# A two-path decoder trunk on one core: the place of a transposition in the last chunk of each feed-forward block, and the pace of a bias table's transfers

## The chip, the cores and the metric

The kernel runs on one core of a Trainium2 chip. The metric is the device time of one execution in microseconds (us), the median of several runs. One further execution was recorded by the hardware profiler; all rows come from it. The engines are TensorE (PE; its weight loads are shown apart as PEld), VectorE (DVE), ScalarE (ACT), GpSimd (POOL) and SyncE (SP, which here only starts transfers). Each has its own queue of instructions and works through it in order.

## The reference, cut to what matters

Two layers over 256 tokens of width 1024. Each layer adds half a feed-forward block (ffn), then a mixer, then half of another ffn. The mixer of the first layer is a diagonal state-space model (S5), that of the second is an attention with three branches over keys and values computed between the layers.

```python
def _swiglu(x, w_in, w_out):
    a, b = jnp.split(x @ w_in, 2, axis=-1)
    return (jax.nn.silu(a) * b) @ w_out
...
for layer in range(DEPTH):
    h = h + 0.5 * _swiglu(_rmsnorm(h, ffn1_norm[layer]), ffn1_w_in[layer], ffn1_w_out[layer])
    u = _rmsnorm(h, mix_norm[layer])
    ...
    h = h + 0.5 * _swiglu(_rmsnorm(h, ffn2_norm[layer]), ffn2_w_in[layer], ffn2_w_out[layer])
    if layer == N_A_LAYERS - 1:
        kv = _shared_kv(...)
```

So four ffns are computed, each with an inner width of 2816. The attention adds to its scores a bias that depends only on the distance of query and key, through 32 buckets of a table `rel_bias` with 16 heads.

## The kernel before

**Products in three passes.** Every float32 matrix is split into a high part (`whi`, rounded, by ACT at L86 or L99) and a low part (`wlo`, the rest, by DVE at L90 or L102; a few by POOL). A product is then three matmuls in `mm3` (L115 to L120): high by high (L118), high by low weights (L119), low by high (L120). Weights come from DRAM as `raw` tiles of 1 MB by `load_granule` (L68), started from SP. `raw` has two buffers, `whi` and `wlo` five of 1024 columns each, so splits run ahead of the matmuls until a buffer is missing.

**A feed-forward block** (`ffn`, L191) goes over 11 chunks (NCH) of 256 inner columns. For each chunk c it computes both halves of the first product for the two token tiles t into two PSUM banks `mm` (48 matmuls over eight k), then `g` = silu(a) * b (ACT L249, DVE L250, for t = 0 and 1). The second product needs `g` with the inner columns on the partitions. `transposed(g)` (L198) does that with four PE transposes (L204) into one bank `tr`, which `split` (L142) copies to `gT` as a high part (ACT L143) and a low part (DVE L144). In the second ffn (`perm`) the split goes in two halves. `second(c, gT)` (L214) then adds 24 matmuls into the four banks `o`: two inner halves f, two output halves hf, two t, three passes. The work is skewed by one chunk: while chunk c's first product runs, the `g` of chunk c - 1 is transposed (after k = 4, L243), and `second(c - 1)` follows the first product of chunk c (L253). After the loop the last chunk is left: L256 transposes its `g` and computes `second(10)`, whose sums L228 adds to `h`; after each sum `done` prepares the next stage.

**The order on each engine.** The source gives each instruction a rank. A scheduler sets the order of each engine's queue when the kernel is built, by rank and by when it expects operands to be ready; on the chip each queue runs in order, with waits on semaphores. An instruction of low rank may thus stand ahead of one of higher rank that was expected to be ready later.

**Background work.** `ffn` can take a generator `bg` with small steps of other work. `background(bg, steps)` (L179) is called after the odd k of each chunk but the first, and at the end of every chunk: call 1 ends chunk 0, and calls 5c - 3 to 5c + 1 lie in chunk c. A step that yields 1 lets the next call go on; a step that yields n counts for n calls. The instructions of a step on ACT, DVE and SP are put behind the latest instructions of the main work on these engines (L185); those on POOL are not.

In the second ffn the background is `bias_tables` (L632). It loads the table and the buckets, multiplies them on PE (L640), and copies the result to `rev` (L643). Then eight transfers, started from POOL, write `rev` 16-fold to a DRAM buffer `revd` (L647, 384 KB each), and one reads it back with overlapping rows as `B` (L652, 2 MB), which the attention uses after the third ffn.

Of the kernel before, what the change touches and what calls it, by code (L numbers as in the profile page):

```python
# [21 lines left out]
NCH = FF // 256  # L22
# [10 lines left out]
def kernel(ctx: ExitStack, tc: tile.TileContext, A, out):  # L33
# [13 lines left out]
    def mm_bank():  # L47
        return Banks.mm.tile([P, 512], F32, name="mm")

    def tr_bank():  # L50
        return Banks.tr.tile([P, 512], F32, name=Banks.tag)
# [55 lines left out]
    def granules(aps, w=512, gain=None, first=(), eng="av"):  # L107
        for n, ap in enumerate(aps):
            raw = first[n] if n < len(first) else load_granule(ap, w)
            for j in range(2):  # L110
                hi, lo = split_half(raw, j, w, gain, ((n % 2) * 2 + j) * 2, eng)
                for s_ in range(2):
                    yield hi[:, s_ * w:(s_ + 1) * w], lo[:, s_ * w:(s_ + 1) * w]

    def mm3(ps, xT, k, t, w, start, stop_):  # L115
        xh, xl = (xT[:, i, k, t * P:(t + 1) * P] for i in range(2))
        wh, wl = w
        T.matmul(ps, lhsT=xh, rhs=wh, start=start, stop=False)  # L118
        T.matmul(ps, lhsT=xh, rhs=wl, start=False, stop=False)  # L119
        Last.pe = T.matmul(ps, lhsT=xl, rhs=wh, start=False, stop=stop_)  # L120

    def gemm(acc, xT, gen, kts=KT, lead=False):

        for k0 in range(0, kts, 4):
            ws = [next(gen) for _ in range(4)] if lead else None
            for t_ in range(2) if lead else (None,):
                for k in range(k0, k0 + 4):
                    w = ws[k - k0] if lead else next(gen)
                    for t in ((t_,) if lead else range(2)):
                        mm3(acc[t], xT, k, t, w, k == 0, k == kts - 1)  # L130
# [11 lines left out]
    def split(dst_hi, dst_lo, src):  # L142
        i = S.activation(dst_hi, src, AF.Copy)  # L143
        V.tensor_tensor(out=dst_lo, in0=src, in1=dst_hi.bitcast(F32), op=ALU.subtract)  # L144
        return i
# [33 lines left out]
    def background(bg, n):  # L179

        if bg is None:
            return
        Pace.left = min(Pace.left, 0.0) + n
        with ExitStack() as st:
            for i in (Last.act, Last.dve, Last.dma):  # L185
                st.enter_context(tc.issue_after(i.ins))
            while Pace.left > 0:
                Pace.left -= next(bg, n) or 1


    def ffn(x, gi, w_in, w_out, res, perm=False, bg=None, steps=1, done=None, first=()):  # L191
        with tc.tile_pool(name="ffn", bufs=2) as fp, tc.tile_pool(name="ps_a", bufs=1, space=PSUM) as pa:
            xT, rs = x.xT, x.rs
            acc2 = [[pa.tile([P, 512], F32, name=f"o{t}{hf}") for hf in range(2)] for t in range(2)]
            g_in = granules([w_in[c, kh] for c in range(NCH) for kh in range(2)], gain=gi, first=first)
            g_out = granules([w_out[j] for j in range(NCH)])

            def transposed(g):  # L198

                gT = fp.tile([P, 2, 2, 256], F32R, name="gT")  # L200
                ps = tr_bank()
                for f in range(2):
                    for t in range(2):
                        T.transpose(ps[:, (f * 2 + t) * P:(f * 2 + t + 1) * P], g[:, t, f * P:(f + 1) * P], ident)  # L204
                if perm:
                    src = ps.rearrange("p (f t e c) -> p f t e c", f=2, t=2, e=2)
                    hi, lo = (gT[:, i].rearrange("p f (c t e) -> p f t e c", t=2, e=2) for i in range(2))
                    for f in range(2):
                        split(hi[:, f], lo[:, f], src[:, f])
                else:  # L210
                    split(gT[:, 0], gT[:, 1], ps.rearrange("p (f c) -> p f c", f=2))
                return gT

            def second(c, gT):  # L214
                if c < NCH - 1:
                    for f in range(2):
                        for hf in range(2):
                            w = next(g_out)
                            for t in range(2):
                                mm3(acc2[t][hf], gT, f, t, w, c + f == 0, False)  # L220
                    return
                ws = [[next(g_out) for _ in range(2)] for _ in range(2)]
                for t in range(2):
                    for hf in range(2):
                        for f in range(2):
                            mm3(acc2[t][hf], gT, f, t, ws[f][hf], False, f == 1)
                        cs = slice(hf * 512, (hf + 1) * 512)
                        V.scalar_tensor_tensor(out=res[:, t, cs], in0=acc2[t][hf], scalar=0.5, in1=res[:, t, cs], op0=ALU.mult, op1=ALU.add)  # L228
                        done(t, hf)

            prev = None
            for c in range(NCH):
                acc = [mm_bank() for _ in range(2)]
                gT = None
                if c == 0:
                    gemm(acc, xT, g_in, lead=True)
                else:
                    for k in range(KT):
                        w = next(g_in)
                        for t in range(2):  # L240
                            mm3(acc[t], xT, k, t, w, k == 0, k == KT - 1)
                        if k == 4:
                            gT = transposed(prev)  # L243
                        if k % 2:
                            background(bg, steps)
                g = fp.tile([P, 2, 256], F32, name="g")
                for t in range(2):
                    sl = g[:, t, :]
                    Last.act = S.activation(sl, acc[t][:, 0:256], AF.Silu, scale=rs[:, t:t + 1])  # L249
                    Last.dve = V.scalar_tensor_tensor(out=g[:, t, :], in0=acc[t][:, 256:512], scalar=rs[:, t:t + 1], in1=sl,  # L250
                                                      op0=ALU.mult, op1=ALU.mult)
                if c:
                    second(c - 1, gT)  # L253
                prev = g
                background(bg, steps)
            second(NCH - 1, transposed(prev))  # L256

# [372 lines left out]
    def bias_tables(kp, tp):  # L632

        rb = tp.tile([32, P], F32, name="rb")
        nc.sync.dma_start(out=rb, in_=A["rel_bias"])
        oh = tp.tile([32, 256], F32, name="oh")
        nc.sync.dma_start(out=oh, in_=A["bucket"])
        yield
        ps = tr_bank()
        T.matmul(ps[:, 0:256], lhsT=rb, rhs=oh, start=True, stop=True)  # L640
        rev = tp.tile([P, 384], F32, name="rev")
        G.memset(rev[:, 256:384], -1e30)
        V.tensor_copy(rev[:, 0:256], ps[:, 0:256])  # L643
        yield
        dr = dscr.tile([8, 16, 16, 384], F32, name="revd")
        for r in range(8):
            nc.gpsimd.dma_start(out=dr[r].rearrange("q h k -> h q k"), in_=rev[r * 16:(r + 1) * 16].unsqueeze(1).to_broadcast([16, 16, 384]))  # L647
            yield
        KV.B = kp.tile([P, 16, 256], F32, name="B")
        a = dr[0]  # L650
        src = bass.AP(tensor=a.tensor, offset=a.offset + 127, ap=[[16 * 384 - 1, P], [384, 16], [1, 256]])
        nc.gpsimd.dma_start(out=KV.B, in_=src)  # L652
        yield
# [351 lines left out]
    with ExitStack() as st:  # L1005
        late = ctx.enter_context(tc.tile_pool(name="late", bufs=1))
        kvp = st.enter_context(tc.tile_pool(name="kvt", bufs=1))
        hd = dscr.tile([256, D], F32, name="hd")
        for i in range(4):
            nc.sync.dma_start(out=hd.rearrange("(c i) d -> i c d", i=4)[i], in_=h[i % 2 * 64:i % 2 * 64 + 64, i // 2, :])  # L1010
        for t in range(2):
            nc.sync.dma_start(out=h[:, t, :], in_=hd[t * P:(t + 1) * P, :])
        kv_consts(kvp)
        ffn(Nxt.x, 1, A["w_in2_0"], A["w_out2_0"], h, perm=True, bg=bias_tables(late, kvp), steps=1, done=fill_next(h))
        x = Nxt.x
        bg = shared_kv(x, late, kvp)
        ffn(x, 3, A["w_in1_1"], A["w_out1_1"], h, bg=bg, steps=1, done=fill_next(h))
# [97 lines left out]
```

## Time and profile before

| | |
|---|---|
| median of 3 runs | 1060.9 us (1058.21 to 1061.9) |
| the profiled execution | 1057.09 us |
| its span, first to last instruction | 1055.3 us |
| mean granted TensorE clock | 0.982 |
| bytes read from DRAM, written | 165.54 MB, 5.24 MB |
| S5 stage, about | 216 to 310 us |
| second ffn, about | 310 to 502 us |
| third ffn with the keys and values ahead of it, about | 502 to 740 us |
| attention, about | 740 to 865 us |
| last ffn, about | 865 to 1055 us |

A row of the timeline has the start in us, the duration, the engine, the line of the kernel, the operation, and out<-in by the program's names; in brackets stand the time that the engine was idle just before and what released it. A row with x2 or x8 joins as many instructions. Matmuls are pipelined, so two that follow each other overlap; the step from one start to the next tells the rate. A row of the waits has the sum of the waits in us, their number and the longest.

### The profile page before, as it was taken

What the parts mean: (1) busy time and instruction counts of PE and PEld (TensorE: products, weight loads), DVE (VectorE), ACT (ScalarE), POOL (GpSimd) and SP (SyncE); (2) the same over time, 40 slices, a digit from 0 to 9 for tenths busy, and PEclk for the clock granted to TensorE, in tenths of its full rate; (3) what the DMA queues carried; (4) which work ended last, traced back from release to release, by engine and by line L of the source; (5) the groups of instructions that cost most, each with busy time, mean ns of one, the idle gap of its engine ahead of it and who ended that gap; (6) DMA issues with size and microseconds to landing.
All of it is one profiled execution on the core that took longest, in us unless ns stands there. A gap on an engine that the chain in (4) does not pass through costs nothing.

```text
span 1055.3 us, 14565 instructions
## 1 busy us (share of the span) xinstructions
PE 996.1 (94%) x5553; PEld 806.6 (76%) x5553; DVE 669.9 (63%) x1258; ACT 583.2 (55%) x1039; POOL 135.8 (13%) x142
## 2 busy tenths in 40 slices
PE   6999999988799799999999999999887999999998
PEld 5888888776577588887887888887865678888886
DVE  4999854367864556566666455555788866556553
ACT  5677675352264555554755555454876755545552
POOL 3001110327611000000013000000205210000000
PEclk9999999989899899999999999999988999999999
DMA  7556554303258755554554455553312145545551
GB/s 256 200 189 211 194 179 147 120 2 112 90 182 240 269 197 179 184 196 160 197 206 156 160 196 170 193 193 115 100 34 91 42 155 199 198 173 188 198 171 70
DMA packets 27910, 171.73 MB, mean 163 GB/s; under 512 B 4544, under 2 KB 4992, under 8 KB 9024
## 3 DMA queue, kind: packets, MB, share of 16 engines
q1 hardware_dynamic: 26192, 164.77, 45.2%
q0 software_dynamic: 1648, 6.03, 2.2%
q8 instruction: 43, 0.70, 0.3%
q14 instruction: 27, 0.22, 0.1%
HBM read 165.54 MB, written 5.24 MB: 162 GB/s over the span
## 4 chain that ended last, share of the span: by engine, by line
PE 80%; DVE 9%; ACT 4%; DMA 3%; POOL 3%; issue 1%; SPq 0%; ACTq 0%; POOLq 0%; DVEq 0%
PE mm L118 15%; PE mm L119 15%; PE mm L120 15%; PE o L118 8%; PE o L119 8%; PE o L120 8%; DMA raw<-in_w_in_dram 3%; PE tr L204 2%; DVE wlo L102 1%; DVE w L542 1%; DVE Pt L904 1%; DVE wlo L90 1%; ACT Pt L893 1%; POOL z L502 1%; PE tr L911 1%
## 5 line engine op out<-in xcount | busy, mean ns | idle before, releaser
L118 PE MATMUL mm<-whi,xT 128*128 128x512 f32 (+2 forms) x800 | 313.3, 392 | 4.0 <-ACT whi L86 2.5
L119 PE MATMUL mm<-wlo,xT 128*128 128x512 f32 (+2 forms) x800 | 306.1, 383 | 0.7 <-DVE wlo L90 0.5
L120 PE MATMUL mm<-whi,xT 128*128 128x512 f32 (+2 forms) x800 | 306.2, 383 | 0.0
L102 DVE SCALAR_TENSOR_TENSOR wlo<-raw,gains,whi 128x512 fp32r<-128x512 f32 (+2 forms) x320 | 221.4, 730 | 111.7 <-ACT whi L99 108.0
L99 ACT ACTIVATE whi<-raw,gains 128x512 fp32r<-128x512 f32 (+2 forms) x320 | 207.4, 694 | 136.1 <-PE mm L120 58.6
L90 DVE TENSOR_TENSOR wlo<-raw,whi 128x1024 fp32r<-128x1024 f32 x140 | 171.0, 1226 | 122.7 <-ACT whi L86 122.6
L86 ACT ACTIVATE whi<-raw 128x1024 fp32r<-128x1024 f32 x148 | 154.5, 1057 | 153.5 <-PE mm L120 58.2
L118 PEld LDWEIGHTS mm<-whi,xT 128*128 128x128 f32 x800 | 150.8, 189 | 35.1 <-ACT whi L86 2.9
L120 PEld LDWEIGHTS mm<-whi,xT 128*128 128x128 f32 x800 | 150.6, 188 | 29.7
L119 PEld LDWEIGHTS mm<-wlo,xT 128*128 128x128 f32 x800 | 150.9, 189 | 28.7 <-DVE wlo L90 1.5
L118 PE MATMUL o<-whi,gT 128*128 128x512 f32 x352 | 140.5, 399 | 10.9 <-ACT gT L143 10.9
L119 PE MATMUL o<-wlo,gT 128*128 128x512 f32 x352 | 139.5, 396 | 0.0
L120 PE MATMUL o<-whi,gT 128*128 128x512 f32 x352 | 138.9, 396 | 0.0
L118 PEld LDWEIGHTS o<-whi,gT 128*128 128x128 f32 x352 | 66.6, 189 | 27.6 <-ACT gT L143 12.6
L120 PEld LDWEIGHTS o<-whi,gT 128*128 128x128 f32 x352 | 66.5, 189 | 16.0 <-DVE gT L144 0.4
L119 PEld LDWEIGHTS o<-wlo,gT 128*128 128x128 f32 x352 | 66.6, 189 | 14.9
L249 ACT ACTIVATE g<-mm,rs 128x256 f32<-128x256 f32 x88 | 41.0, 471 | 28.2 <-PE mm L120 27.9
L250 DVE SCALAR_TENSOR_TENSOR g<-mm,rs,g 128x256 f32<-128x256 f32 x88 | 41.8, 481 | 22.5 <-ACT g L249 22.4
L144 DVE TENSOR_TENSOR gT<-tr,gT 128x512 fp32r<-128x512 f32 (+1 forms) x55 | 36.4, 663 | 27.4 <-ACT gT L143 27.0
L143 ACT ACTIVATE gT<-tr 128x512 fp32r<-128x512 f32 (+1 forms) x55 | 33.3, 606 | 36.1 <-PE tr L204 29.3
L140 POOL TENSOR_TENSOR rs<-ms,nhalf 128x1 f32<-128x1 f32 x12 | 7.2, 600 | 219.9 <-DVE ms L139 219.9
L893 ACT ACTIVATE Pt<-Pt,mx 128x128 f32<-128x128 f32 (+1 forms) x64 | 28.4, 445 | 6.4 <-DVE mx L888 6.4
(300 smaller groups left out, 985.2 us busy)
## 6 DMA issues: line engine op xcount, KB each, us to landing
raw<-in_w_in_dram SPq DMA_DIRECT2D x87, 1024.0 KB, 4.9
raw<-in_w_out_dram SPq DMA_DIRECT2D x44, 1024.0 KB, 4.9
raw<-in_w_kv_dram SPq DMA_DIRECT2D x6, 1024.0 KB, 4.8
raw<-in_w_glu_dram SPq DMA_DIRECT2D x4, 1024.0 KB, 4.8
raw<-in_w_o_dram SPq DMA_DIRECT2D x4, 1024.0 KB, 4.8
revd<-rev POOLq DMA_DIRECT2D x8, 384.0 KB, 16.2
raw<-in_w_qg_dram SPq DMA_DIRECT2D x6, 512.0 KB, 3.5
B<-revd POOLq DMA_DIRECT2D x1, 2048.0 KB, 10.9
```

Of the source, the lines that this page charges most:

```text
L86: Last.act = S.activation(hi, r, AF.Copy)
L90: Last.dve = V.tensor_tensor(out=lo, in0=r, in1=hi.bitcast(F32), op=ALU.subtract)
L99: Last.act = S.activation(hi[:, c], r[:, c], AF.Identity, scale=g_)
L102: i = V.scalar_tensor_tensor(out=lo[:, c], in0=r[:, c], scalar=g_, in1=hi[:, c].bitcast(F32), op0=ALU.mult, op1=ALU.subtract)
L118: T.matmul(ps, lhsT=xh, rhs=wh, start=start, stop=False)
L119: T.matmul(ps, lhsT=xh, rhs=wl, start=False, stop=False)
L120: Last.pe = T.matmul(ps, lhsT=xl, rhs=wh, start=False, stop=stop_)
L143: i = S.activation(dst_hi, src, AF.Copy)
L144: V.tensor_tensor(out=dst_lo, in0=src, in1=dst_hi.bitcast(F32), op=ALU.subtract)
L249: Last.act = S.activation(sl, acc[t][:, 0:256], AF.Silu, scale=rs[:, t:t + 1])
L250: Last.dve = V.scalar_tensor_tensor(out=g[:, t, :], in0=acc[t][:, 256:512], scalar=rs[:, t:t + 1], in1=sl, op0=ALU.mult, op1=ALU.mult)
L893: S.activation(Pt[:, r, br], Pt[:, r, br], AF.Exp, scale=-1.0, bias=mx[:, c:c + 1], accum_out=sm[:, c:c + 1])
```

## The change

`second` gets a parameter `fs`, the inner halves that it computes. In the last chunk, c = 10, the 24 matmuls of `second(9)` are divided: f = 0, then the transposition of the chunk's own `g`, then f = 1. After the loop `second(10)` takes the `gT` made there. In `bias_tables` each of the eight transfers yields 5 instead of 1.

```diff
-            def second(c, gT):
+            def second(c, gT, fs=(0, 1)):
                 if c < NCH - 1:
-                    for f in range(2):
+                    for f in fs:
                         for hf in range(2):
                             w = next(g_out)
                             for t in range(2):
...
-                if c:
+                if c == NCH - 1:
+                    second(c - 1, gT, (0,))
+                    last = transposed(g)
+                    second(c - 1, gT, (1,))
+                elif c:
                     second(c - 1, gT)
                 prev = g
                 background(bg, steps)
-            second(NCH - 1, transposed(prev))
+            second(NCH - 1, last)
...
         for r in range(8):
             nc.gpsimd.dma_start(out=dr[r].rearrange("q h k -> h q k"), in_=rev[r * 16:(r + 1) * 16].unsqueeze(1).to_broadcast([16, 16, 384]))
-            yield
+            yield 5
```

## The prediction

> **What bounds the kernel now.** I read the page first (engines, chain), then the costliest groups, then the waits of TensorE (PE) stage by stage, and last the timeline around each wait.
>
> ```profile
> span 1055.3 us, 14565 instructions
> PE 996.1 (94%) x5553; PEld 806.6 (76%) x5553; DVE 669.9 (63%) x1258; ACT 583.2 (55%) x1039; POOL 135.8 (13%) x142
> ...
> PE 80%; DVE 9%; ACT 4%; DMA 3%; POOL 3%; issue 1%; SPq 0%; ACTq 0%; POOLq 0%; DVEq 0%
> ...
> L118 PE MATMUL o<-whi,gT 128*128 128x512 f32 x352 | 140.5, 399 | 10.9 <-ACT gT L143 10.9
> ```
>
> PE is busy 94% of the span and carries 80% of the chain that ended last, so an edit is worth the PE idle time that it takes away, and little else. The last row names such idle time: the first matmuls into `o` (the second product of a feed-forward block, ffn) stood idle 10.9 us, all of it until ACT had copied the transposed gate product `gT`. Five waits make it up: one at the end of each ffn and one long one in the second chunk of the second ffn. The change touches both kinds. The profiled execution took 1057.09 us, of which the span is 1055.3; the median of the three runs is 1060.9. I work out the change in us on the profiled execution and take it off the median.
>
> **Part one: the transposition in the last chunk.** The end of the last ffn, in the timeline:
>
> ```profile
> 1038.47 0.40 PE L118 MATMUL o<-whi,gT 128*128 128x512 f32 x1
> ...
> 1039.18 0.48 DVE L250 SCALAR_TENSOR_TENSOR g<-mm,rs,g 128x256 f32<-128x256 f32 x1 [0.20 <-ACT g L249]
> ...
> 1043.84 0.40 PE L120 MATMUL o<-whi,gT 128*128 128x512 f32 x1
> 1044.08 0.60 PE L204 MATMUL tr<-ident,g 128*128 128x128 f32 x4
> 1044.71 0.60 ACT L143 ACTIVATE gT<-tr 128x512 fp32r<-128x512 f32 x1 [5.56 <-PE tr L204]
> 1045.34 0.69 DVE L144 TENSOR_TENSOR gT<-tr,gT 128x512 fp32r<-128x512 f32 x1 [5.68 <-ACT gT L143]
> 1045.36 0.50 PE L118 MATMUL o<-whi,gT 128*128 128x512 f32 x1 [0.69 <-ACT gT L143]
> 1045.70 0.39 PE L119 MATMUL o<-wlo,gT 128*128 128x512 f32 x1
> ```
>
> The 24 matmuls of `second(9)` start at 1038.47, and the last of them at 1043.84, a step of 5.37/23 = 0.233 us. Then come four transposes, the copy on ACT, and only then the next product. The subtraction on DVE runs beside the matmuls that need only the high half. PE shows 0.69 us idle. The same rows at the other three ends (first, second and third ffn), and then the same four transposes inside a chunk, where 18 ready matmuls follow them:
>
> ```profile
> 206.97 0.39 PE L120 MATMUL o<-whi,gT 128*128 128x512 f32 x1
> ...
> 208.83 0.39 PE L119 MATMUL o<-wlo,gT 128*128 128x512 f32 x1
> ```
>
> ```profile
> 492.54 0.39 PE L120 MATMUL o<-whi,gT 128*128 128x512 f32 x1
> ...
> 494.64 0.39 PE L119 MATMUL o<-wlo,gT 128*128 128x512 f32 x1
> ```
>
> ```profile
> 731.30 0.39 PE L120 MATMUL o<-whi,gT 128*128 128x512 f32 x1
> ...
> 733.58 0.40 PE L119 MATMUL o<-wlo,gT 128*128 128x512 f32 x1
> ```
>
> ```profile
> 1033.67 0.39 PE L120 MATMUL mm<-whi,xT 128*128 128x512 f32 x1
> ...
> 1033.90 0.60 PE L204 MATMUL tr<-ident,g 128*128 128x128 f32 x4
> ...
> 1034.57 0.40 PE L119 MATMUL mm<-wlo,xT 128*128 128x512 f32 x1
> ```
>
> From the last L120 before the transposes to the second matmul after them passes 1.86, 2.10, 2.28 and 1.86 us at the four ends, 8.10 in all. Inside the chunk it is 0.90. The change puts the transposes inside: 12 matmuls of `second(9)` stand ahead of them and 12 behind, so they cost what they cost in the chunk. No matmul, transpose, copy or load is added or dropped. The gain is 8.10 - 4 x 0.90 = 4.50 us. The lower bound from these rows for a fully hidden copy is its idle time alone, some 0.7 us at the plainest end, 2.8 for four; the upper bound is everything beyond two ordinary matmul steps, 8.10 - 4 x 0.47 = 6.2. I take 4.5, since the row inside the chunk is the same operation in the place to which it is moved.
>
> What has to hold for it. (a) `g` must be there when 12 matmuls are through: DVE finishes it at 1039.18 + 0.48 = 1039.66, and 12 steps from 1038.47 end at 1041.27, a margin of 1.6 us. The transposes are a new wait in PE's queue, with the 12 matmuls behind them; by this margin nothing stands. (b) The copy must be done when the other 12 are through. Transposes from 1041.27, ACT until about 1042.5, DVE until about 1043.2; the 12 matmuls end at 1041.27 + 0.44 + 2.8 = 1044.5. That leaves 2.0 us for the high half and 1.3 for the low one. (c) ACT and DVE must not be held up by the splits of the next stage's weights, which run in the second and third of these ends:
>
> ```profile
> 490.22 1.34 ACT L99 ACTIVATE whi<-raw,gains 128x512 fp32r<-128x512 f32 x2 [1.17 <-PE o L120]
> 493.02 0.72 ACT L99 ACTIVATE whi<-raw,gains 128x512 fp32r<-128x512 f32 x1 [1.46 <-PE o L120]
> ...
> 495.09 0.64 ACT L143 ACTIVATE gT<-tr 128x256 fp32r<-128x256 f32 x1 [0.36 <-DVE gT L144]
> ```
>
> ```profile
> 728.92 0.99 ACT L99 ACTIVATE whi<-raw,gains 128x304 fp32r<-128x304 f32 x2 [1.46 <-PE o L120]
> 731.73 0.99 ACT L99 ACTIVATE whi<-raw,gains 128x304 fp32r<-128x304 f32 x2 [1.82 <-PE o L120]
> 732.62 0.57 ACT L143 ACTIVATE gT<-tr 128x512 fp32r<-128x512 f32 x1
> ```
>
> At 731.73 a pair of splits stands ahead of the copy, which is why that end costs 2.28. In the new place the pair of 728.92 stands ahead instead: by steps of 0.234 back from 731.30 the first 12 matmuls end near 728.7, ACT is free at 729.9, the copy is done by 730.5 and DVE by 731.2, before PE gets through at 732.0. In the second ffn the copy goes in two halves that wait for each other (ACT, DVE, ACT, DVE). There the last ACT copy began 2.55 us after the last L120 (492.54 to 495.09), splits in between. Counted from 489.73, where the twelfth matmul starts, it begins at 492.3 and, with 0.64 on ACT and as much on DVE, is done at 493.6, or at 494.9 if the pair of 490.22 (1.34) comes on top. The first matmul that needs its low half is the sixth after the 24, at 493.2 + 5 x 0.233 = 494.4, so up to 0.5 us can stay. What is late next is the matmuls themselves: all that follows an end (the sum into `h`, the next fill) hangs on PE's last matmul and moves up with it.
>
> **Part two: `yield 5`.** It lets five calls of the background pass between two transfers of the bias table: the eight calls 3 to 10 (chunks 1 and 2) become 3, 8, ... 38 (one in each of chunks 1 to 8), and the load of `B` goes from call 11 to call 43, in chunk 9. The long wait lies just there:
>
> ```profile
> 319.90 4.55 POOL L647 DMA_DIRECT2D revd<-rev  x8 [5.51 <-DVE rev L643]
> 345.31 1.17 POOL L652 DMA_DIRECT2D B<-revd  x1 [20.85 <-DMA revd<-rev]
> 347.97 1.33 ACT L99 ACTIVATE whi<-raw,gains 128x512 fp32r<-128x512 f32 x2 [7.39 <-DMA raw<-in_w_in_dram]
> 349.21 0.61 ACT L143 ACTIVATE gT<-tr 128x256 fp32r<-128x256 f32 x1
> 349.87 0.79 PE L118 MATMUL o<-whi,gT 128*128 128x512 f32 x1 [7.51 <-ACT gT L143]
> ...
> 352.60 0.46 PE L118 MATMUL o<-whi,gT 128*128 128x512 f32 x1
> ```
>
> ```profile
> 327.00:342.00 15.00, 14.87 (x68) 11.85 (x66) 5.29 (x7) 4.57 (x6) 0.00 (x0) 1.00 0.98 312
> 342.00:350.00 8.00, 0.49 (x3) 0.13 (x1) 1.30 (x3) 1.85 (x3) 1.17 (x1) 0.74 0.94 328
> ...
> 358.00:374.00 16.00, 16.00 (x73) 13.12 (x72) 10.15 (x14) 9.19 (x14) 0.00 (x0) 1.00 0.54 193
> ```
>
> The columns of the last fence are the stretch, its length, the busy time of PE, PEld, DVE, ACT and POOL, the granted clock, the DMA share and GB/s. Eight transfers fill the DMA engines (0.98 against 0.54 after), a weight load comes late, ACT sits on its split, the copy of `gT` is queued behind that split, and PE waits 7.51 us.
>
> But by the rows the position in the source doesn't hold these transfers. Two of the old calls are 12 matmuls apart, 12 x 0.23 = 2.7 us, and the eight reach from chunk 1 to the last of chunk 2; yet the eight issues took 4.55 us, 0.57 each, back to back. POOL is a queue of its own. The background hangs its ACT, DVE and SP instructions behind the last ones of the main work, and a POOL transfer behind nothing but `rev`. POOL runs ahead of the source elsewhere too:
>
> ```profile
> 298.00 0.53 POOL L763 MEMSET hvt<- 128x512 f32 x1
> ```
>
> This memset belongs to the background of the third ffn, and the second ends only after the row of 494.64. Between 319.90 and the end of this ffn POOL has no other work than these nine transfers, so a later rank passes nothing. I take 0. The bounds are 0 and the whole stall: 7.5 us of gap (PE stood from 349.87 - 7.51 = 342.36), and the six matmul steps from 349.87 to 352.60 took 2.73 instead of 6 x 0.233 = 1.40, another 1.3; together 8.8.
>
> [...]
>
> **The sum.** 4.50 + 0 = 4.5 us: span 1050.8, profiled execution 1052.6, median 1060.9 - 4.5 = 1056.4 us (-0.42%).
>
> **Rivals.** *The wait moves to ACT.* At the second and third ends the copy may be queued behind a split that waits for one of the last of the 12 matmuls (as at 493.02 and 731.73); then these two give nothing, and 2 x 0.96 = 1.9 us is left: 1059.0. For it: ACT runs in order, and it was so there before. Against it: the transposes are ready 3 us earlier than these splits' buffers.
>
> *The transfers do spread*, so part two does what it says: another 8.8, 1056.4 - 8.8 = 1047.6 us. For it: the stall is real and is caused by the eight at once. Against it: the 0.57 us spacing above.
>
> [...]
>
> *Slower: a second block in ACT.* The place is the end of the third ffn, where splits read a load that has just come:
>
> ```profile
> 725.74 5.11 SPq L70 DMA_DIRECT2D raw<-in_w_qg_dram  x2
> ```
>
> ```profile
> raw<-in_w_qg_dram SPq DMA_DIRECT2D x2, 608.0 KB, 3.7
> ```
>
> It lands near 729.4 and is wanted at 731.73. If the new order of ACT sets such a split ahead of the copy and the load comes over 2.5 us later than usual, after 732.0, PE stands as from 342.36 to 349.87. The price is up to 8.8 us against the gain of 4.5: 1056.4 + 8.8 = 1065.2. For it: one such block is in this trace. Against it: that one needed the DMA engines full, and no POOL transfer runs near 730. The instruction order is drawn anew by a scheduler, so the same could happen elsewhere; I count that here.
>
> **How the numbers follow.** Forecast 0.70, the wait on ACT 0.12, spread 0.09, slower 0.09. About 0.3% (3.2 us) is what a measurement of this kernel can tell from no change. Of the forecast's 0.70 I put 0.50 over 3.2 us of gain and 0.20 under it, for the 0.5 that may stay in the second ffn and the lower bound of 2.8. Faster 0.50 + 0.09 = 0.59; within 0.20 + 0.12 = 0.32; slower 0.09. The forecast's own range is 1054.7 (6.2 us) to 1058.1 (2.8). With the ACT case that is 0.82 at best, and the runs alone spread by 3.7 us, so I go on to the spread case: 1047 to 1060.5.
>
> **What would show it.** In the trace after: four transposes L204 between two groups of 12 matmuls into `o` at each end, no PE wait on `gT` at the four ends, and 0.90 from L120 to L119 across the transposes. The eight transfers still 0.57 us apart, the 7.5 us wait still there. Wrong would be: transfers one per chunk; a PE wait on L143 at an end; a PE wait on L204's `g` in front of the transposes; or a new wait over 2 us anywhere in 740 to 865.

## The result and the profile after

| | before | after |
|---|---|---|
| median, 14 runs each on the same chip | 1060.55 us (1057.27 to 1062.93) | 1059.97 us (1056.32 to 1064.3) |
| ratio, 95% interval | | 0.9996 (0.9982 to 1.0010) |
| the profiled execution, its span | 1057.09, 1055.3 us | 1061.53, 1059.8 us |

By this interval the change lies between 1.9 us less and 1.1 us more: no change that can be measured, where 4.5 us less was forecast. A single execution varies by some 3 us to either side, so that the spans of the two profiled ones say nothing by themselves; their stages do. The page of the kernel after, its span, its engines and the group of the first products into `o`:

```profile
span 1059.8 us, 14565 instructions
...
PE 999.1 (94%) x5553; PEld 809.7 (76%) x5553; DVE 674.7 (64%) x1258; ACT 582.8 (55%) x1039; POOL 134.0 (13%) x142
...
L118 PE MATMUL o<-whi,gT 128*128 128x512 f32 x352 | 140.6, 400 | 8.6 <-ACT gT L143 8.6
```

The idle time on `gT` was 10.9 us in five waits. It is 8.6 now, and the waits of PE (sum, number, longest) count it as a single one: all four waits at the ends are gone, and the long one of the second ffn is still there.

```profile
PE o L118 <- ACT gT L143: 8.6, 1, 8.6
```

Lines behind the change have moved by 4 (L870 was L866); in the variants below by a little more or less.

**The ends**, in PE's timeline of the kernel after:

```profile
204.93 0.39 PE L120 MATMUL o<-whi,gT 128*128 128x512 f32 x1
...
205.83 0.40 PE L119 MATMUL o<-wlo,gT 128*128 128x512 f32 x1
...
491.54 0.39 PE L120 MATMUL o<-whi,gT 128*128 128x512 f32 x1
...
492.44 0.39 PE L119 MATMUL o<-wlo,gT 128*128 128x512 f32 x1
...
729.22 0.39 PE L120 MATMUL o<-whi,gT 128*128 128x512 f32 x1
...
730.12 0.39 PE L119 MATMUL o<-wlo,gT 128*128 128x512 f32 x1
...
735.03 0.40 PE L119 MATMUL o<-wlo,gT 128*128 128x512 f32 x1
735.27 0.60 PE L159 MATMUL tr<-ident,h 128*128 128x128 f32 x4
735.62 0.48 PE L120 MATMUL o<-whi,gT 128*128 128x512 f32 x1
...
1046.42 0.40 PE L120 MATMUL o<-whi,gT 128*128 128x512 f32 x1
...
1047.32 0.40 PE L119 MATMUL o<-wlo,gT 128*128 128x512 f32 x1
```

From L120 to L119 across the transposes pass 0.90 us at each of the four ends, and matmuls stand on both sides. The time from the first matmul of `second(9)` to the last of `second(10)` fell by 0.95, 0.62, 0.93 and 0.95 us. At the second and third ends one group of L159 more (four transposes for the next `xT`) now lies inside this stretch, where it stood behind it; the rows 735.03 to 735.62 show what such a group adds, 0.59 - 0.23 = 0.36 us (0.48 at the second end). With these two the ends give 0.95 + 1.10 + 1.29 + 0.95 = 4.3 us.

**The transfers**, in the timeline of POOL (a DMA issued by it is a row):

```profile
319.70 4.55 POOL L651 DMA_DIRECT2D revd<-rev  x8 [4.82 <-DVE rev L647]
346.16 1.17 POOL L656 DMA_DIRECT2D B<-revd  x1 [21.91 <-DMA revd<-rev]
```

Eight issues in 4.55 us, back to back, as before.

**The attention.** So the gain at the ends is there, and yet it is not in the time. It was lost in the stage behind the third end. The stretch from the last matmul of the third ffn into `o` to the last matmul of the attention's output product, and ten microseconds of it (stretch, length, busy time of PE, PEld, DVE, ACT and POOL, granted clock, DMA share, GB/s), before:

```profile
739.70:862.00 122.30, 105.50 (x658) 82.36 (x656) 95.19 (x353) 84.45 (x244) 29.45 (x28) 0.94 0.25 83
839.70:849.70 10.00, 9.08 (x48) 6.40 (x47) 6.75 (x9) 5.19 (x9) 7.62 (x6) 1.00 0.41 125
```

and after:

```profile
739.50:867.40 127.90, 108.62 (x654) 84.72 (x652) 97.54 (x352) 83.65 (x243) 30.03 (x28) 0.92 0.25 79
839.50:849.50 10.00, 6.35 (x27) 4.72 (x25) 8.91 (x10) 3.27 (x5) 7.79 (x6) 0.73 0.43 127
```

122.3 us have become 127.9, 5.6 more, at a clock of 0.92 instead of 0.94. Nothing of the change is in this stage. But the waits of PE here are others (line waited for, us in all, times, the longest), before, from 735 to 890:

```profile
PE tr L866 <- DVE pst L144: 5.3, 2, 4.5
PE s L882 <- DVE clg L890: 4.6, 4, 2.4
PE s L882 <- ACT qT L847: 1.9, 1, 1.9
```

and after:

```profile
PE s L886 <- DVE clg L894: 4.7, 3, 1.8
PE tr L870 <- DVE pst L144: 3.8, 2, 3.6
PE tr L870 <- DVE hms L671: 3.7, 1, 3.7
PE mm L118 <- ACT whi L99: 3.3, 1, 3.3
```

The instructions are the same ones; their order in the queues is not. Set side by side, the queues of the two kernels differ at the four ends, as they should, and then throughout the attention on PE, DVE, ACT and POOL. At the third end the trace shows the beginning: ACT copies `gT` behind four splits of the queries' weights (727.21, 729.65, then 730.54), where it came behind six (726.49, 728.92, 731.73, then 732.62). From there on the scheduler has drawn another order. Only some groups of waits are shown here; all of them sum to 16.4 us before and 19.2 after.

**Theory (A).** The change does at the ends what the prediction says, and is worth nothing in the bias tables. What takes the gain back is the order of the attention, which moving the third end draws anew. **Rival (B):** the third end's transposition itself costs, by standing in the way of the next stage. A second question is what the long wait of the second ffn would be worth if the transfers did spread. (In the expectations below A and B stand for the two theories that each names.)

### The profile page after: what moved, and what is told of

Read it like the earlier page. It is cut to its first block, busy times and chain, and to the rows that moved or that the text cites. A ratio compares the mean times of both kernels' runs of the same rounds, so it can differ in the third digit from the quotient of the medians.

```text
span 1059.8 us, 14565 instructions
## 1 busy us (share of the span) xinstructions
PE 999.1 (94%) x5553; PEld 809.7 (76%) x5553; DVE 674.7 (64%) x1258; ACT 582.8 (55%) x1039; POOL 134.0 (13%) x142
## 4 chain that ended last, share of the span: by engine, by line
PE 74%; DVE 13%; DMA 5%; ACT 3%; POOL 2%; issue 2%; SPq 0%; ACTq 0%; POOLq 0%; DVEq 0%
PE mm L118 14%; PE mm L119 14%; PE mm L120 14%; PE o L120 7%; PE o L118 7%; PE o L119 7%; DMA raw<-in_w_in_dram 4%; DVE wlo L90 3%; PE tr L204 1%; DVE Pt L908 1%; DVE wlo L102 1%; DVE w L546 1%; PE tr L915 1%; ACT whi L86 1%; DVE WBT L280 1%
## 5 line engine op out<-in xcount | busy, mean ns | idle before, releaser
L119 PE MATMUL mm<-wlo,xT 128*128 128x512 f32 (+2 forms) x800 | 306.7, 384 | 0.6 <-DVE wlo L90 0.5
L120 PE MATMUL mm<-whi,xT 128*128 128x512 f32 (+2 forms) x800 | 306.6, 384 | 0.0
L102 DVE SCALAR_TENSOR_TENSOR wlo<-raw,gains,whi 128x512 fp32r<-128x512 f32 (+2 forms) x320 | 221.8, 730 | 114.0 <-ACT whi L99 109.9
L99 ACT ACTIVATE whi<-raw,gains 128x512 fp32r<-128x512 f32 (+2 forms) x320 | 207.2, 694 | 136.2 <-PE mm L120 58.9
L120 PEld LDWEIGHTS mm<-whi,xT 128*128 128x128 f32 x800 | 151.2, 189 | 29.7
L119 PEld LDWEIGHTS mm<-wlo,xT 128*128 128x128 f32 x800 | 151.5, 189 | 28.6 <-DVE wlo L90 1.5
L119 PE MATMUL o<-wlo,gT 128*128 128x512 f32 x352 | 140.4, 399 | 0.0
L120 PE MATMUL o<-whi,gT 128*128 128x512 f32 x352 | 140.0, 398 | 0.2 <-DVE gT L144 0.2
L120 PEld LDWEIGHTS o<-whi,gT 128*128 128x128 f32 x352 | 66.8, 190 | 16.5 <-DVE gT L144 1.0
L119 PEld LDWEIGHTS o<-wlo,gT 128*128 128x128 f32 x352 | 66.8, 190 | 15.0
```

Of the source, the lines that this page charges most:

```text
L99: Last.act = S.activation(hi[:, c], r[:, c], AF.Identity, scale=g_)
L102: i = V.scalar_tensor_tensor(out=lo[:, c], in0=r[:, c], scalar=g_, in1=hi[:, c].bitcast(F32), op0=ALU.mult, op1=ALU.subtract)
```

## The experiments

**One part at a time.** The first kernel has `yield 5` alone. The second and third have the transposition moved in some ffns only, by a flag `mid`:

```diff
-            yield
+            yield 5
```

```diff
-                if c:
+                if mid and c == NCH - 1:
+                    second(c - 1, gT, (0,))
+                    last = transposed(g)
+                    second(c - 1, gT, (1,))
+                elif c:
...
-            second(NCH - 1, transposed(prev))
+            second(NCH - 1, last if mid else transposed(prev))
```

> The kernel before with yield 5 alone. Theory: a POOL transfer is held by nothing in the main work, and the order of all five queues is the same as before, so ratio 1.000 within the interval, eight issues 0.57 us apart, the wait of 7 to 9 us on gT in the second chunk of the second ffn still there. It also shows how far two kernels with equal queues stand apart in such a measurement. Rival (the transfers do spread): 0.9917 (-8.8 us), one issue per chunk.

> The transposition moved at the ends of the first, second and fourth ffn, not of the third; yield as before. The queues of the attention keep their old order. Theory (the moved transposition gives what it should, and the attention's redrawn order takes it back): the three ends measured 0.95, 0.6 and 0.95 us in the trace of the changed kernel, so -2.5 us, ratio 0.9976, and attention as long as before. Rival (each end's gain is lost again in the stage that follows it, whatever the order): only the last end counts, -0.95 us, ratio 0.999.

> The transposition moved at the end of the third ffn alone; yield as before. All queues of the attention are in the new order. Theory (redrawn order): the end gains 0.9 us, the attention loses more; with the changed kernel at -0.6 and ends 1, 2, 4 at -2.5, this is +1.9 us, ratio 1.0018, and stretch 740 to 865 longer by some 3 us or more. Rival (the longer attention in the profile was a chance of that execution): -0.9 us, ratio 0.9991.

| | median us | ratio to before, 95% interval |
|---|---|---|
| `yield 5` alone | 1060.2 | 0.9994 (0.9978 to 1.0011) |
| ends 1, 2 and 4 | 1056.54 | 0.9962 (0.9944 to 0.9979) |
| end 3 alone | 1062.64 | 1.0017 (1.0000 to 1.0034) |

`yield 5` does nothing: its five queues hold the same instructions in the same order as before, and its long wait is 8.1 us. The three ends outside the attention bring 4.0 us (2.2 to 5.9), against 0.95 + 1.10 + 0.95 = 3.0 by their rows; in that kernel the attention has its old order. The third end alone gains by its rows and makes the kernel no faster; its attention is the redrawn one, with the waits on L671 and L99 of 3.7 and 3.3 us, and takes 125.9 us. A single execution tells the length of this stretch only to some 3 us: in the eight profiles of this document in which the attention has its old order, it takes 121.3 to 124.5 us, 122.9 on the mean. The two with the change's order, 125.9 and 127.9, lie above all of them, by 4.0 on the mean. The loss goes with the third end, but these runs don't tell the order from the transposition.

**The order without the third end.** Two kernels hold the first weight splits of the attention behind the last fill of `xT`, which draws the attention's order anew (not the same as the change's). The first has the third end as before, the second as in the change. In both the attention's queues are the same but for a few places at its start.

```diff
-                    Q[b_[0]] = queries(*b_)
+                    with (tc.issue_after(Last.fill.ins) if b_[0] in (0,) else ExitStack()):
+                        Q[b_[0]] = queries(*b_)
```

> Kernel before with all four ends as they were; only the first weight splits of the attention's queries are put behind the last fill of xT, so that the scheduler draws the attention's order anew (another order than that of the change, and without the third end in it). Theory A (the attention's order alone moves the time by a few us, whatever the third end does): ratio differs from 1 by 0.002 or more, to either side. Theory B (the order does not matter, the third end's own transposition costs): ratio 1.000.

> As the one before, with the third end as in the change; the attention then has the same order in all five queues in both kernels, so that their difference is the third end alone. Theory A: 0.9 us less than that kernel (the 0.93 us measured between second(9) and the last product at the third end), a ratio 0.001 lower. Theory B: 1 to 2 us more than that kernel, a ratio 0.001 to 0.002 higher.

The ratios are 1.0105 (1.0088 to 1.0122) with the old third end and 1.0096 (1.0072 to 1.0119) with the new one. The same stretch as above, with the old third end:

```profile
743.20:877.00 133.80, 112.58 (x657) 87.06 (x656) 100.72 (x359) 86.83 (x250) 29.95 (x28) 0.90 0.25 79
```

and with the new one:

```profile
740.30:873.20 132.90, 111.52 (x654) 86.53 (x652) 100.63 (x358) 86.81 (x250) 29.96 (x28) 0.90 0.24 80
```

With no transposition moved, another order of the attention costs 11.1 us, and the stretch is 11.5 us longer. So the order can outweigh the whole change, as theory A says. It is not the order alone, though: the edit holds the splits back, and in this kernel PE waits 5.8 us for them (4.4 for `whi` of L99, 1.4 for `wlo` of L102), where before it waited for no split in this stage. That the third end gains under an equal order is what its rows say (1.29 us); the difference of the two runs has that sign, 0.0009, but lies inside their intervals. Theory B's 0.001 to 0.002 the other way is not seen, and not excluded by these two runs either; a kernel below speaks to it.

**What in the order.** The last wait for `pst` shows it best, near 840 us. (Before, the two waits for `pst` sum to 5.3 us, but 4.5 of them are an earlier one, at 802.61; in the order of after PE waits 3.65 us for L671 at that place, 800.55.) DVE's timeline of the kernel after, and the one row of POOL beside it:

```profile
839.43 4.20 DVE L908 TENSOR_SCALAR Pt<-Pt,sm 128x256 f32<-128x256 f32 x4
843.55 1.34 DVE L144 TENSOR_TENSOR pst<-clg,pst 128x120 fp32r<-128x120 f32 x1
```

```profile
839.52 7.79 POOL L95 TENSOR_TENSOR wlo<-raw,whi 128x512 fp32r<-128x512 f32 x6 [20.61 <-ACT whi L86]
```

PE's timeline at the same place:

```profile
840.90 0.39 PE L118 MATMUL x<-whi,oT 128*128 128x512 f32 x1
844.94 1.11 PE L870 MATMUL tr<-ident,pst 128*128 128x128 f32 x4 [3.65 <-DVE pst L144]
```

While POOL subtracts (1.30 us each), a scaling on DVE takes 4.20/4 = 1.05 us on the mean and the low part of `pst` 1.34; in a kernel below, where POOL has no subtraction at this place, each takes 0.28. Four scalings stand ahead of `pst`, so PE waits 3.65 us, and its clock falls: the four transposes take 1.11 us (0.66 in the kernel before, at 841.38), the ten microseconds have a clock of 0.73. (With the third end alone a wait of 3.6 us for `pst` is there too, and that stage was 2 us shorter, at a clock of 0.95.) In the order of before the scalings ahead of `pst` are done when POOL begins; DVE, then POOL:

```profile
839.15 0.87 DVE L904 TENSOR_SCALAR Pt<-Pt,sm 128x256 f32<-128x256 f32 x3
839.99 1.33 DVE L144 TENSOR_TENSOR pst<-clg,pst 128x120 fp32r<-128x120 f32 x1
841.25 2.67 DVE L904 TENSOR_SCALAR Pt<-Pt,sm 128x256 f32<-128x256 f32 x2
```

```profile
839.91 7.62 POOL L95 TENSOR_TENSOR wlo<-raw,whi 128x512 fp32r<-128x512 f32 x6 [21.09 <-ACT whi L86]
```

There PE waited 0.84 us. Two kernels take the cause away: the last three low parts of the output weights go from POOL to DVE, in the kernel after, and in the fastest one so far (below). The queues are otherwise the same but for some places beside them.

```diff
-                hi, lo = split_half(raw, j, w, gain, ((n % 2) * 2 + j) * 2, eng)
+                hi, lo = split_half(raw, j, w, gain, ((n % 2) * 2 + j) * 2, 'av' if n * 2 + j >= 5 else eng)
```

> Kernel of the change, with the last three low parts of the attention's output weights (wlo of w_o) on VectorE instead of GpSimd; the queues are the same otherwise but for a few places beside them. Theory A (in the change's order four scalings of Pt and the low part of pst stand in VectorE's queue just where GpSimd subtracts, take 1.05 and 1.34 us instead of 0.3, and so let TensorE wait 3.65 us for pst at 845 and grow cold): scalings of 128x256 between 835 and 850 under 0.4 us each, the 3.65 us wait gone, 3 to 5 us less than the change, ratio to the kernel before 0.995 to 0.997. Theory B (these scalings are long for another reason, or the loss lies elsewhere in the redrawn attention): scalings still about 1 us, ratio 1.000; three low parts of 1.23 us more on VectorE then make it up to 1.003.

The ratio is 0.9948 (0.9932 to 0.9964), 1054.78 us against 1059.92 of before on that chip. DVE's timeline of this kernel:

```profile
839.93 1.22 DVE L90 TENSOR_TENSOR wlo<-raw,whi 128x1024 fp32r<-128x1024 f32 x1
841.06 0.28 DVE L144 TENSOR_TENSOR pst<-clg,pst 128x120 fp32r<-128x120 f32 x1
841.26 1.93 DVE L908 TENSOR_SCALAR Pt<-Pt,sm 128x256 f32<-128x256 f32 x7
```

and its stretches, as above:

```profile
739.90:861.50 121.60, 105.94 (x653) 82.74 (x652) 94.67 (x355) 83.55 (x243) 22.24 (x22) 0.94 0.25 83
839.90:849.90 10.00, 9.88 (x52) 7.07 (x51) 7.99 (x16) 5.01 (x9) 0.00 (x0) 1.00 0.57 194
```

A scaling takes 1.93/7 = 0.28 us, `pst` 0.28, the clock stays at 1.00, and the attention is back at 121.6 us, 6.3 less than after, 3.6 of it idle time of PE (19.3 to 15.7) and the rest its busy time (108.62 to 105.94), at a clock of 0.94 instead of 0.92. The order beside `pst` has changed as well: one low part of 1.22 us now stands ahead of it in the place of the four scalings. But four scalings at 0.28 would take 1.12, as long, so by this estimate it was the length of the scalings and not their place alone that made PE wait. With the cause gone the change shows: 1 - 0.9948 is 5.5 us (3.8 to 7.2), about the 4.3 of its ends and the 0.7 that the attention is now under before (in one execution each). The third end is moved in this kernel too, and it is no slower than the one with ends 1, 2 and 4 (0.9962), so rival B, that the third end's transposition itself costs, does not hold.

**The long wait of the second ffn.** `yield 5` holds no transfer back. In the next kernel each waits for the newest `g`, by a copy of one column on POOL:

```diff
+            mk = G.tensor_copy(mark, Last.g[:, 1, 0:1])
+            with tc.issue_after(mk.ins):
-            nc.gpsimd.dma_start(out=dr[r].rearrange("q h k -> h q k"), in_=...)
-            yield
+                nc.gpsimd.dma_start(out=dr[r].rearrange("q h k -> h q k"), in_=...)
+            yield 5
```

> The kernel before with yield 5 and a small POOL copy of one column of the latest g ahead of each POOL transfer of the bias tables, so that the copy's wait on g holds the transfer; only the POOL queue changes. Theory (eight transfers at once cause the long wait, and spread they would hide): issues one per chunk, some 16.6 us apart, the wait on gT of 7.5 us gone, -8.8 us, ratio 0.9917. Rival (each transfer delays the weight load beside it and PE pays every time): eight waits of 1 us or more, or one of several us where B is loaded, ratio 1.000 or above.

The ratio is 0.9968 (0.9952 to 0.9984), 3.4 us less where 8.8 were expected. POOL's timeline:

```profile
320.79 0.65 POOL L654 DMA_DIRECT2D revd<-rev  x1 [4.92 <-DVE rev L647]
...
328.11 0.59 POOL L654 DMA_DIRECT2D revd<-rev  x1
346.58 0.57 POOL L654 DMA_DIRECT2D revd<-rev  x1
```

and the waits of PE from 310 to 502:

```profile
PE o L118 <- ACT gT L143: 5.0, 8, 1.5
```

The transfers go one per chunk, and the long wait is gone. One of the eight waits, 0.94 us, is the end of the ffn; in the place of the long one seven chunks wait 0.2 to 1.5 us, 4.1 in all: half of the stall was spread, not removed. Eight loads of `w_in`, each issued some 2 us behind a transfer, take 8.2 to 10.3 us there, against a median of 5.0 for all 87 of this kernel. Is the queue of ACT to blame, where the copy of `gT` stands behind a split that waits for its load, or the late load? The next two kernels put, in the second ffn, the splits of the weights that follow in the source behind the copy in ACT's queue (the edit binds ACT alone; DVE follows it), with bunched and with held transfers.

```diff
-                        w = next(g_in)
+                        with tc.issue_after(gta.ins) if gta and perm else ExitStack():
+                            w = next(g_in)
...
                             gT = transposed(prev)
+                            gta = Last.gt
```

> Kernel before, but in the second ffn the copies of a transposed gate product (gT) stand ahead of the weight splits that follow them in the source, in ScalarE's and VectorE's queues; the transfers stay bunched. Theory A (the 7.5 us wait is a queue's: the copy of gT stands in ScalarE's queue behind the split of a weight that is late because eight transfers crowd the DMA queues): the wait on gT at 342 us falls from 7.5 us to under 2 and the cold stretch of clock behind it goes, about 7 us less, ratio 0.993. Theory B (the late weights themselves set the pace, the wait on gT only stands where PE feels it first): PE waits as long on the next weights instead, ratio 0.999 to 1.000.

> As the one with the copies ahead, and the transfers held to one per chunk. If the queue alone makes the stall (A), the held transfers have nothing left to give and each chunk's 0.6 us on gT falls as well: ratio 0.992 to 0.993. If late weights set the pace (B), the waits on gT of each chunk turn into waits on weights: ratio 0.997, as with the held transfers alone.

The ratios are 1.0175 (1.0149 to 1.0201) and 1.0066 (1.0040 to 1.0092): both slower. The waits of PE from 310 to 530, bunched:

```profile
PE mm L118 <- ACT whi L99: 19.9, 11, 8.8
```

and held:

```profile
PE mm L118 <- ACT whi L99: 11.2, 10, 1.1
```

The wait has changed its name: bunched, PE stands 8.8 us for the weights where it stood 7.5 for `gT`. That is what theory B expects to see, but it is not the same late load. SyncE's loads of `w_in` in the kernel before, then SyncE and ACT in the bunched one:

```profile
313.95 7.93 SPq L70 DMA_DIRECT2D raw<-in_w_in_dram  x2
```

```profile
323.35 4.19 SPq L70 DMA_DIRECT2D raw<-in_w_in_dram  x2
```

```profile
338.96 2.56 ACT L99 ACTIVATE whi<-raw,gains 128x512 fp32r<-128x512 f32 x4 [13.16 <-DMA raw<-in_w_in_dram]
```

A held split keeps its `raw` buffer: SyncE waited 12.9 us for a low part of L102, and so the edit itself put off the load, from 313.95, ahead of the transfers, to 323.35, among them. So these two kernels do not decide between A and B. By the rows of before A remains likely: with the copy of `gT` ahead PE could have run the 24 matmuls of 0.23 us, 5.6 us, from 342.36 to about 348, when the split of the late load began (347.97); that is an estimate, and no run shows it. In both kernels ten chunks pay about 1.1 us each (19.9 - 8.8 = 11.1, and 11.2), as a split that waits for the copy comes too late for the matmuls; held, the loads of `w_in` in these chunks take only 4.8 to 6.6 us. Neither theory had foreseen that price; the old order, splits first, was the better one.

**Together.** Ends 1, 2 and 4 and held transfers; the same with the copies ahead; and the first of these with the three low parts on DVE.

> Ends 1, 2 and 4 as in the change, the third as before, and the transfers of the bias tables held to one per chunk. Theory (the two gains lie in different places and add): 4.0 + 3.4 = 7.4 us less than before, ratio 0.993, 1053.1 us. Rival (the second end's transposition was only worth something because the stall stood ahead of it, or the held transfers reach into the second end): no better than the better of the two alone, ratio 0.996.

> Ends 1, 2 and 4 as in the change, copies of gT ahead in the second ffn, transfers held. If A holds: 4.0 us of the ends and about 7 of the second ffn, ratio 0.989 to 0.990 (1049 to 1050 us). If B holds: 7.4 us, ratio 0.993, as without the copies ahead.

> Ends 1, 2 and 4 as in the change, transfers held, the attention in the order of the kernel before, and the last three low parts of w_o on VectorE. By theory A there is little left to gain here: in this order three scalings are done before GpSimd begins and TensorE waits only 0.84 us for pst; the ratio stays at 0.994 (0.993 to 0.995). By theory B with VectorE as the bound the three low parts cost up to 3.7 us, ratio 0.997.

| | median us | ratio to before, 95% interval |
|---|---|---|
| ends and held transfers | 1053.18 | 0.9942 (0.9922 to 0.9962) |
| and copies ahead | 1063.38 | 1.0036 (1.0018 to 1.0053) |
| ends, held, low parts on DVE | 1052.68 | 0.9936 (0.9915 to 0.9958) |

The two gains add (0.9962 x 0.9968 = 0.9930, inside the interval), the copies ahead lose again, and in the old order of the attention the low parts on DVE are worth nothing that shows. That answers to theory A: the same edit brings 5 us where the order sets four of DVE's scalings ahead of `pst` under POOL's subtractions, and nothing that shows where it doesn't. The last row has the lowest ratio of all, though not by more than the intervals; all four ends with held transfers and low parts on DVE was not tried.

## Why the prediction was wrong on the time

**Part one at the ends: right.** The four ends cost 0.90 us each, as said, which by the prediction's own rows is 8.10 - 3.60 = 4.50; the stretches give 4.3. All three conditions held. `g` was there: no wait stands ahead of L204. The copy was done: no wait on `gT` at an end. And of ACT's splits at the third end just the pair stands ahead of the copy that was named (729.65, the copy at 730.54). The rival of a wait on ACT did not come, nor the 0.5 us that might have stayed in the second ffn.

**Part two: right.** No transfer moved, and `yield 5` alone measures 0.9994. The upper bound of 8.8 us was too high even for transfers that do spread: they gave 3.4, as loads behind the transfers still come late (8.2 to 10.3 us) and seven chunks still wait, 4.1 us in all.

**The step that failed** is the sentence "all that follows an end [...] hangs on PE's last matmul and moves up with it". It takes the order of what follows as given. Behind the third end it was not: the attention was drawn anew and took some 4.0 us more (125.9 with the third end alone, 127.9 with the whole change, against 121.3 to 124.5 in the old order), about as much as the ends had given. The prediction's own sign of it came true, "a new wait over 2 us anywhere in 740 to 865": 3.7 us for L671, 3.3 for L99, and 3.65 for `pst` where 0.84 was before. It held this for possible ("The instruction order is drawn anew by a scheduler"), but inside a rival of 0.09, priced by a late load at 730 that did not occur. Experiments show both halves: the same stage in another order with no end moved costs 11 us, 5.8 of it waits for the splits that the edit held back; the change without POOL's last six subtractions beside DVE's scalings gains 5.5.

The measured 1059.97 us lies inside the range on record, 1047 to 1060.5, and outside the forecast's own, 1054.7 to 1058.1. That it lies inside is luck: the range was carried up to 1060.5 for a wait on ACT at two ends (1059.0) and for the spread of the runs, and neither is what brought the time there.

**What stays open.** What tips the scheduler at the third end, and not at the others, is not shown. The waits for L671 and L99 (3.7 and 3.2 us) stand in the change's kernel with the low parts on DVE as well, whose attention is as short as before, so that they weigh no more than the old waits that they replaced; of the three new waits the one for `pst` made the loss. Of the 11 us of the other order the 5.8 of the held splits are named, not the rest. Whether ACT's queue or the late load makes the long wait of the second ffn is open.

## What to carry to other kernels

Where a scheduler sets the order, price an edit in two parts: its own rows, and the chance that the stage behind it is drawn anew; the second was as large here as the first. Try a local edit place by place, and set the queues of the two kernels side by side before believing a gain or a loss. When a good edit brings nothing, look in the stage that it does not touch for an instruction that has become several times as long, and for what runs beside it.

## What the runs showed of the hardware

**DVE and POOL.** All 32 scalings of 128x256 in the attention, with POOL's last six subtractions beside them and without; the kernel after, then the one with the low parts on DVE:

```profile
L908 DVE TENSOR_SCALAR Pt<-Pt,sm 128x256 f32<-128x256 f32 x32 | 14.5, 505 | 0.1
```

```profile
L908 DVE TENSOR_SCALAR Pt<-Pt,sm 128x256 f32<-128x256 f32 x32 | 9.3, 348 | 0.1
```

A scaling under a subtraction takes up to 1.38 us (the longest of its kind), about the 1.30 us of one subtraction on POOL. The extra length goes away with the subtraction (0.28 above); by what way the one holds up the other, no row shows.

**The clock after a short gap.** PE's timeline of the kernel after, behind the wait for L99:

```profile
768.92 0.80 PE L118 MATMUL mm<-whi,xT 128*128 128x256 f32 x2 [3.25 <-ACT whi L99]
...
771.96 0.41 PE L119 MATMUL mm<-wlo,xT 128*128 128x256 f32 x1
772.17 0.36 PE L120 MATMUL mm<-whi,xT 128*128 128x256 f32 x1
772.37 0.28 PE L118 MATMUL mm<-whi,xT 128*128 128x256 f32 x1
772.49 0.28 PE L119 MATMUL mm<-wlo,xT 128*128 128x256 f32 x1
```

A gap of 3.25 us is followed by 3.3 us of steps of 0.21 instead of 0.12, at a granted clock of 0.50 (768.91 to 772.32); by these steps it costs another 3.3 x 0.09/0.21 = 1.4 us, an estimate. In the profiles of before and after the eight gaps of PE of 3.25 to 8.62 us, those at the very start left out, each have a stretch with a granted clock of 0.50 at them, of 3.4, 6.8 or 10.2 us. Equal gaps do not bring equal stretches: in the kernel after the 3.65 us for L671 come with 10.2 us (799.63 to 809.87), the 3.65 for `pst` with 6.8 (844.01 to 850.84).
